# Splitting the gated activations behind the value rows, and a last normalization scaled by VectorE alone

## The chip, the cores and the metric

The kernel runs on one core of a Trainium2 chip. The metric is the device time of one execution in microseconds (us), taken as the median of several runs. Engines are named as the profile names them: PE is TensorE (PEld its weight loads), DVE is VectorE, ACT is ScalarE, POOL is GpSimd, SP is SyncE, which here only issues transfers. Transfers run on 16 DMA engines. SBUF is the memory on the core that all engines read, PSUM the one into which TensorE adds up.

## The reference

One decoder layer over 256 tokens of width 2048, in fp32. The change lies in its last part, a lookup of experts (PEER) and the normalization behind it. Each token has 8 heads; each picks the best 16 of 128 x 128 experts, and an expert is a single neuron with one row of `u` and one of `v`:

```python
    ue = u[eidx]
    h = jnp.einsum('cd,chkd->chk', xc, ue).astype(jnp.float32)
    a = jax.nn.gelu(h, approximate=False) * g
    ve = v[eidx]
    return jnp.einsum('chk,chkd->cd', a.astype(ve.dtype), ve)
...
    # the layer ends with
    x <- LayerNorm(ALPHA * x + PEER(x))
```

`a` is called the gated activation below: the gelu of a token's product with an expert's row, times the gate `g`. What lies ahead (a combined projection, two attentions, an output projection and a first normalization) is not touched.

## The kernel before, in words

**Products in fp32.** A matrix product is made from parts: a number is cast to a short form (the high part: `wh`, `ah`) and the rest is a subtraction (the low part: `wl`, `al`). ScalarE casts, VectorE subtracts, and TensorE adds up high x high, low x high and high x low. The helper `split` (L146) does both for small tiles, `split_half` for 1024 of the 2048 columns of a row tile.

**Experts in blocks.** Experts that tokens chose are put into columns: a block is 128 experts, one per partition, whose rows of `u` or `v` (128x2048, 1.049 MB) POOL gathers by a list of indices. Where a block serves both token tiles (t = 0 and 1, 128 tokens each) it is worked with all 256 tokens, else with the half that needs it. Blocks have a part: C and D, and the "singles" S0 and S1 (28 of them), in which each expert serves exactly one token.

**Units.** The program is a list of units; each needs one row tile of 1.049 MB. `run_units` works through them in order. The last 110 are the value units (rows of `v`), numbered u0 to u109 here; u0 begins near 1220 us. Their order alternates: a block for both tiles (24 matmuls of 128x512), then a single (8 matmuls) or a block for one tile (12 matmuls), with some changes; u101 is the last that adds to tile t = 0, and u102 to u109, the tail, are blocks of one half for t = 1. TensorE adds all of it up in eight banks of PSUM, four for each t. A unit has four steps s = 0 to 3, one for each 512 columns.

**What each unit needs, and who makes it.**

- its rows, `raw` or `rawv` (three buffers each, used in turn), gathered up to six units ahead on POOL (`dma_unit`); then `wh` by ScalarE and `wl` by VectorE in two halves, one unit ahead (`split_ahead`, called at each step; the halves are due at s = 0 and s = 2).
- its activations: `ar` comes from DRAM (`load_a`: SP for blocks of C, POOL's gather for D) and the gates `gr` by a gather on POOL, both four units ahead. `split_a(k + 2)`, called at s = 0, multiplies `ar` by `gr` on VectorE, casts it to `ah` on ScalarE and subtracts `al` on VectorE; for a single it writes the mask `one` instead, which says which token each expert serves.
- a single also needs its activations `acts`: the generator `job_singles` gathers its row of `u` and its token's row (`sr`, 1.049 MB each, four buffers, so two singles at a time), multiplies and sums them on VectorE, and, once per seven singles, gathers seven tiles of gates (`gsr`) and reduces them on VectorE to `gate` and `token`.

**What sets the order.** The program's order on each engine is the order in which Python calls the instructions; nothing is reordered later. All compute goes through a wrapper (`Paced`), so that every compute instruction has line L116; gathers have L187. The wrapper also keeps a model clock for each engine while the program is written down. Background work (`job_singles`; `job_ln2`, the normalization of tile t = 0) consists of generators. After each step, `pump` advances them if the clocks allow it: not if the model's ScalarE or VectorE is too far ahead of its TensorE, and not before the job's own due time. So a call that is made at another place in a step moves the clocks, and with them the places of the jobs' instructions. An engine works strictly in its order; an instruction that waits holds up all behind it, on POOL and SP the transfers' issues.

**The end.** When the last block of a tile has been added up, `residual` adds the four banks to ALPHA times the layer's input (`yacc`) and takes statistics of each 512 columns (`bn_stats`). `ln_stats` combines them (`bn_aggr`) and makes the reciprocal square root with small instructions. The scaling of 512 columns is either `ln2_a` and `ln2_b` (two VectorE instructions) or `ln2_pool` (one on ScalarE, two on POOL); each ends with the output's transfer. For t = 0 `job_ln2` takes columns 2 and 3 with VectorE and 0 and 1 with ScalarE and POOL. For t = 1, behind all units, the order before is: `ln_stats`, one scalar product (`ln2_start`), column block 3 by ScalarE and POOL, blocks 1, 2 and 0 by VectorE. The names `g2b2` are the normalization's weights, broadcast to two buffers of `sr`.

Of the kernel before, what the change touches and what calls it, by code (L numbers as in the profile page):

```python
# [17 lines left out]
OP = mybir.AluOpType  # L18
AX = mybir.AxisListType

P = 128
S = 256
# [99 lines left out]
def layer_kernel(ctx: ExitStack, tc: tile.TileContext, xT, x, win, wo, wq, ut, un, v, lams, sublng,  # L122
# [6 lines left out]
    SP = nc.sync  # L129
# [32 lines left out]
    units = []  # L162
# [60 lines left out]
    def split_ahead(k, s):  # L223
        if k + 1 < len(units) and units[k + 1]["kind"] == "C":
            turn_quarter(k + 1, s)
        for at, ahead, i in units[k]["at"]:
            if at == s and k + ahead < len(units) and units[k + ahead]["kind"] != "C":
                split_half(k + ahead, i)
# [3 lines left out]
    def start(gen):  # L232
        jobs.append([0.0, gen])
# [34 lines left out]
    def run_units(upto, slack=SLACK):  # L268


        while pos["k"] < upto:
            k = pos["k"]
            if k == 0:
                load_first()
                for _ in range(2):
                    dma_unit()
                for i in range(2):
                    split_half(1, i)
            if k == 2:
                load_consts()  # L280
            if k == 4:
                make_consts()
            u = units[k]
            clk["now"] = clk["PE"]
            n_late = len(later)
            for s, _ in enumerate(u["use"](u)):
                if s == 0:
                    if k >= n_c - 4:
                        load_a(k + 4)
                    while st["dma"] <= min(k + (6 if "vx" in keep else 3), len(units) - 1):  # L290
                        dma_unit()
                    if k >= n_c - 2:
                        split_a(k + 2)
                split_ahead(k, s)
                for f in later[:n_late]:
                    f()
                del later[:n_late]
                pump(slack)
                clk["now"] = clk["PE"]
                n_late = len(later)  # L300
            pos["k"] = k + 1
# [455 lines left out]
    def ln_stats(pool, t):  # L757

        mv[t] = pool.tile([P, 2], F32, name="mv", tag=f"mv{t}")
        rstd[t] = r = pool.tile([P, 4], F32, name="rstd", tag=f"rstd{t}")  # L760
        v, y, m, w = (r[:, i:i + 1] for i in range(4))
        DVE.bn_aggr(out=mv[t], in_=bst[t])
        DVE.tensor_scalar(v, mv[t][:, 1:2], EPS, None, op0=OP.add)
        DVE.tensor_scalar(y.bitcast(I32), v.bitcast(I32), 1, None, op0=OP.logical_shift_right)
        DVE.tensor_scalar(m, v, -0.5, None, op0=OP.mult)
        DVE.tensor_scalar(y.bitcast(I32), y.bitcast(I32), -1.0, RSQRT_MAGIC, op0=OP.mult, op1=OP.add)
        for _ in range(3):
            DVE.scalar_tensor_tensor(w, y, m, y, op0=OP.mult, op1=OP.mult)
            DVE.scalar_tensor_tensor(y, w, 1.5, y, op0=OP.add, op1=OP.mult)
# [462 lines left out]
    def cols_of(halves):  # L1232
        return slice(halves[0] * P, (halves[-1] + 1) * P)
# [116 lines left out]
                gather(u["a"], hd, hidx[:, c:c + 1])  # L1350
            gather(u["g"], gtab, column(aidx, u["part"], u["b"]))

    def split_a(k):
        if k >= n_all:
            return
        u = units[k]
        if u["kind"] == "S":
            u["ah"] = ex.tile([P, P], F32R, name="one", tag="one", bufs=2)
            DVE.tensor_scalar(u["ah"], row, token[:, u["s"]:u["s"] + 1], None, op0=OP.is_equal)
            return  # L1360
        u["ah"] = ex.tile([P, S], F32R, name="ah", tag="ah", bufs=3)
        u["al"] = ex.tile([P, S], F32R, name="al", tag="al", bufs=3)
        c = cols_of(u["halves"])
        DVE.tensor_tensor(u["a"][:, c], u["a"][:, c], u["g"][:, c], op=OP.mult)
        split(u["ah"][:, c], u["al"][:, c], u["a"][:, c])

    yps = {}
# [1 line left out]
    def use_v(n, single, halves):  # L1369
        def use(u):  # L1370
            for t in halves:
                if t not in yps:
                    yps[t] = [psA() if t == 0 else psB() for _ in range(4)]
            h, l = u["h"], u["l"]
            for c in range(4):
                vs = slice(c * 512, (c + 1) * 512)
                for t in halves:
                    ts = slice(t * P, (t + 1) * P)
                    o = (n == first_of[t], n == last_of[t])
                    if single:  # L1380
                        ops = ((u["ah"], h), (u["ah"], l))
                    else:
                        ops = ((u["ah"][:, ts], h), (u["ah"][:, ts], l), (u["al"][:, ts], h))
                    for i, (a, z) in enumerate(ops):
                        PE.matmul(yps[t][c], a, z[:, vs], start=o[0] and i == 0, stop=o[1] and i == len(ops) - 1)
                    if o[1]:
                        residual(t, c, yps[t][c])
                        if t == 0 and c == 3:
                            start(job_ln2())
                yield  # L1390
        return use

# [19 lines left out]
    def ln2_a(t, db):  # L1412
        y = ycols(t, db)
        c = slice(db * 512, (db + 1) * 512)
        DVE.scalar_tensor_tensor(y, y, mv[t][:, 0:1], g2b2[0][:, c], op0=OP.subtract, op1=OP.mult)

    def ln2_b(t, db):
        y = ycols(t, db)
        c = slice(db * 512, (db + 1) * 512)
        DVE.scalar_tensor_tensor(y, y, rstd[t][:, 1:2], g2b2[1][:, c], op0=OP.mult, op1=OP.add)  # L1420
        SP.dma_start(out[t * P:(t + 1) * P, c], y)

    def ln2_start(t):

        DVE.scalar_tensor_tensor(rstd[t][:, 2:3], mv[t][:, 0:1], -1.0, rstd[t][:, 1:2], op0=OP.mult, op1=OP.mult)

    def ln2_pool(t, db):
        y = ycols(t, db)
        c = slice(db * 512, (db + 1) * 512)
        ACT.activation(y, y, AF.Identity, scale=rstd[t][:, 1:2], bias=rstd[t][:, 2:3])  # L1430
        POOL.tensor_tensor(y, y, g2b2[0][:, c], op=OP.mult)
        POOL.tensor_tensor(y, y, g2b2[1][:, c], op=OP.add)
        (ACT if t else SP).dma_start(out[t * P:(t + 1) * P, c], y)

    def job_ln2():
        yield
        ln_stats(ex, 0)
        ln2_start(0)
        while not g2b2:
            yield  # L1440
        for db in (2, 3):
            yield
            ln2_a(0, db)
            ln2_b(0, db)
        while st["dma"] < n_all or st["a"] < n_all:
            yield
        for db in range(2):
            ln2_pool(0, db)
            yield
# [110 lines left out]
    keep["vx"] = ctx.enter_context(tc.tile_pool(name="vx", bufs=1, side="right"))  # L1560
    run_units(n_all, SLACK_VALUES)
    drain()
    ln_stats(ex, 1)
    ln2_start(1)
    ln2_pool(1, 3)
    for db in (1, 2):
        ln2_a(1, db)
    for db in (1, 2):
        ln2_b(1, db)
    ln2_a(1, 0)  # L1570
    ln2_b(1, 0)


    again = nc.values_load(flag[0:1, 0:1], min_val=0, max_val=1)
# [98 lines left out]
```

## Time and profile before

| what | value |
|---|---|
| median of 3 runs | 1713.2 us (1708.8 to 1714.13) |
| profiled execution | 1714.49 us, span 1712.4 us, mean granted clock 0.96 |
| PE busy | 1580.7 us, 92% of the span |
| DVE, ACT, POOL busy | 1285.7, 815.8, 599.5 us |
| moved by DMA | 409.19 MB, mean 239 GB/s |

The span is the time from the profile's first to its last instruction. Busy shares are means over stages that have different limits: the value units begin near 1220 us and the last matmul ends near 1693, and of these stretches of 100 us and less are shown below. In the rows of a timeline the first two numbers are the start and the duration in us; "x2" says that two instructions of a kind were put together; what stands in brackets at the end is how long the engine was idle before, and whose end released it. In the rows of waits the numbers are: us in total, times, the longest one.

### The profile page before, as it was taken

Reading aid. Unit: us, or ns where it says so; the run is one execution under the profiler, and the core shown is the slowest. Engines: PE = TensorE matmul, PEld = TensorE weight load, DVE = VectorE, ACT = ScalarE, POOL = GpSimd, SP = SyncE. Lnnn points to the kernel's source line nnn. Section 1 sums busy time; section 2 is a strip of 40 time slices with the busy share of each in tenths; the row PEclk is TensorE's granted clock in tenths of the full one; section 3 lists DMA queues with packets and bytes.
Section 4 is the critical chain, followed back from the end, with each engine's and each line's share of the span. In section 5 each row is a group of like instructions: output and inputs, shape, how many; then the busy total and the mean of one; then the engine's idle time right before and its main releaser. Section 6 shows DMA issues by size and latency. Waiting matters only on the chain.

```text
span 1712.4 us, 25292 instructions
## 1 busy us (share of the span) xinstructions
PE 1580.7 (92%) x9151; PEld 1334.9 (78%) x9151; DVE 1285.7 (75%) x2908; ACT 815.8 (48%) x1370; POOL 599.5 (35%) x557
## 2 busy tenths in 40 slices
PE   7999999998999899969798889999889999999994
PEld 5888888876888688759687778898858777788872
DVE  5686767665999898867956567776768888877767
ACT  5445555445433575315544324344445555555533
POOL 0033100004878500001010143344466666556742
PEclk9999999998999899979899899999999999999998
DMA  7454454555444446825147688798999999988861
GB/s 278 163 183 141 155 175 149 217 197 186 162 148 155 175 140 224 280 83 185 55 139 240 203 321 321 264 384 324 376 352 406 390 385 388 371 325 310 302 253 56
DMA packets 112532, 409.19 MB, mean 239 GB/s; under 512 B 11216, under 2 KB 62608, under 8 KB 69648
## 3 DMA queue, kind: packets, MB, share of 16 engines
q0 software_dynamic: 37856, 246.96, 38.0%
q1 hardware_dynamic: 74400, 160.27, 27.4%
q8 instruction: 74, 1.21, 0.3%
q14 instruction: 58, 0.48, 0.1%
q10 hardware_dynamic: 144, 0.26, 0.0%
HBM read 376.00 MB, written 31.39 MB: 238 GB/s over the span
## 4 chain that ended last, share of the span: by engine, by line
PE 67%; DVE 19%; DMA 5%; issue 3%; ACT 3%; POOL 1%; SPq 0%; DVEq 0%; ACTq 0%; POOLq 0%
PE psa L116 34%; PE psb L116 34%; DVE wl L116 6%; DVE oh L116 2%; ACT wh L116 2%; DVE og L116 1%; DVE lw L116 1%; DMA raw<-in_v_dram,vidx 1%; DVE ti L116 1%; DVE yacc L116 1%; DMA raw<-in_win_dram 1%; DMA raw<-in_un_dram,vidx 1%; DVE tv L116 1%; DVE eid L116 1%; DVE cand L116 1%
## 5 line engine op out<-in xcount | busy, mean ns | idle before, releaser
L116 PE MATMUL psb<-xx,wh 128*128 128x512 f32 (+1 forms) x1407 | 510.6, 397 | 0.3 <-issue 0.3
L116 DVE TENSOR_TENSOR wl<-raw,wh 128x1024 fp32r<-128x1024 f32 (+2 forms) x278 | 321.7, 1172 | 104.2 <-ACT wh L116 97.6
L116 PE MATMUL psb<-xx,wl 128*128 128x256 f32 x1392 | 376.7, 285 | 3.8 <-DVE wl L116 2.1
L116 ACT CAST wh<-raw 128x1024 fp32r<-128x1024 f32 (+1 forms) x278 | 283.6, 1045 | 69.2 <-PE psa L116 26.4
L116 PEld LDWEIGHTS psb<-xx,wh 128*128 128x128 f32 x1407 | 270.7, 194 | 37.6 <-issue 0.5
L116 PE MATMUL psa<-xx,wh 128*128 128x512 f32 x800 | 289.1, 405 | 9.3 <-DVE xx L116 8.0
L116 PEld LDWEIGHTS psb<-xx,wl 128*128 128x128 f32 x1392 | 269.8, 194 | 8.5 <-DVE wl L116 2.4
L187 POOL DMA_INDIRECT raw<-in_un_dram,vidx x54 | 59.6, 1103 | 457.8 <-PE psa L116 242.6
L116 PE MATMUL psa<-xx,wl 128*128 128x256 f32 x800 | 218.3, 283 | 1.0 <-DVE wl L116 0.8
L116 DVE TENSOR_TENSOR wl<-psa,wh 128x512 fp32r<-128x512 f32 x216 | 146.7, 687 | 89.3 <-ACT wh L116 78.5
L116 ACT CAST wh<-psa 128x512 fp32r<-128x512 f32 x216 | 126.7, 589 | 161.4 <-PE psa L116 145.2
L116 PEld LDWEIGHTS psa<-xx,wh 128*128 128x128 f32 x800 | 149.9, 191 | 42.8 <-ACT wh L116 9.9
L116 PEld LDWEIGHTS psa<-xx,wl 128*128 128x128 f32 x800 | 152.8, 191 | 7.0 <-DVE wl L116 2.4
L116 DVE TENSOR_TENSOR wl<-rawv,wh 128x1024 fp32r<-128x1024 f32 x106 | 125.7, 1222 | 28.4 <-ACT wh L116 22.5
L116 PE MATMUL psa<-ident,raw 128*128 128x128 f32 x864 | 133.1, 276 | 5.4 <-DMA raw<-in_un_dram,vidx 4.3
L116 ACT CAST ah<-ar 128x256 fp32r<-128x256 f32 (+1 forms) x82 | 30.3, 370 | 203.1 <-DVE ar L116 174.1
L116 PE MATMUL psb<-wl,ah 128*128 128x512 f32 x276 | 110.4, 400 | 7.2 <-DVE wl L116 7.2
L116 PEld LDWEIGHTS psa<-ident,raw 128*128 128x128 f32 x864 | 105.0, 143 | 15.0 <-issue 6.3
L116 PE MATMUL psa<-wh,ah 128*128 128x512 f32 x268 | 107.1, 400 | 5.1 <-ACT wh L116 5.1
L116 PE MATMUL psb<-wh,ah 128*128 128x512 f32 x276 | 110.3, 400 | 1.5 <-DVE bl L116 0.8
L116 PE MATMUL psa<-wl,ah 128*128 128x512 f32 x268 | 107.7, 402 | 4.1 <-DVE wl L116 3.2
L116 PE MATMUL psb<-wh,al 128*128 128x512 f32 x276 | 109.4, 396 | 0.0
(303 smaller groups left out, 2948.6 us busy)
## 6 DMA issues: line engine op xcount, KB each, us to landing
raw<-in_win_dram SPq DMA_DIRECT2D x42, 1024.0 KB
raw<-in_ut_dram SPq DMA_DIRECT2D x32, 1024.0 KB
raw<-in_wo_dram SPq DMA_DIRECT2D x18, 1024.0 KB
raw<-in_wq_dram SPq DMA_DIRECT2D x16, 1024.0 KB
gtab<-stg SPq DMA_DIRECT2D x32, 512.0 KB
cdr<-bl SPq DMA_DIRECT2D x39, 128.0 KB
ar<-cdr SPq DMA_DIRECT2D x39, 128.0 KB
hd<-bl SPq DMA_DIRECT2D x32, 128.0 KB
```

Source lines behind the costliest of these rows:

```text
L116: return f(*a, **k)
L187: nc.gpsimd.indirect_dma_start(dst, None, src, bass.IndirectOffsetOnAxis(ap=index, axis=0))
```

## The change

The function `split_a` is cut in two. `gated` (at s = 0, as before) holds the product `ar` x `gr` or a single's mask; `split_a`, with the cast `ah` and the subtraction `al`, is called at s = 2 behind `split_ahead`, so that it stands behind both halves of the row split made in that unit. `ln_stats` for t = 1 is called directly behind the last `residual`. All of tile t = 1 is scaled by VectorE, a block's two instructions one behind the other, and the outputs of blocks 1 and 3 are issued by ScalarE. The number of matmuls and their order do not change.

```diff
@@ run_units
                     if k >= n_c - 2:
-                        split_a(k + 2)
+                        gated(k + 2)
                 split_ahead(k, s)
+                if s == 2 and k >= n_c - 2:
+                    split_a(k + 2)
                 for f in later[:n_late]:
                     f()
@@
-    def split_a(k):
+    def gated(k):
         if k >= n_all:
             return
         u = units[k]
...
             DVE.tensor_scalar(u["ah"], row, token[:, u["s"]:u["s"] + 1], None, op0=OP.is_equal)
             return
+        c = cols_of(u["halves"])
+        DVE.tensor_tensor(u["a"][:, c], u["a"][:, c], u["g"][:, c], op=OP.mult)
+
+    def split_a(k):
+        if k >= n_all or units[k]["kind"] == "S":
+            return
+        u = units[k]
         u["ah"] = ex.tile([P, S], F32R, name="ah", tag="ah", bufs=3)
         u["al"] = ex.tile([P, S], F32R, name="al", tag="al", bufs=3)
         c = cols_of(u["halves"])
-        DVE.tensor_tensor(u["a"][:, c], u["a"][:, c], u["g"][:, c], op=OP.mult)
         split(u["ah"][:, c], u["al"][:, c], u["a"][:, c])
@@ use_v
                         if t == 0 and c == 3:
                             start(job_ln2())
+                        elif c == 3:
+                            ln_stats(ex, 1)
@@ ln2_b
-        SP.dma_start(out[t * P:(t + 1) * P, c], y)
+        (ACT if t and db % 2 else SP).dma_start(out[t * P:(t + 1) * P, c], y)
@@ behind run_units(n_all, SLACK_VALUES)
     drain()
-    ln_stats(ex, 1)
-    ln2_start(1)
-    ln2_pool(1, 3)
-    for db in (1, 2):
+    for db in range(4):
         ln2_a(1, db)
-    for db in (1, 2):
         ln2_b(1, db)
-    ln2_a(1, 0)
-    ln2_b(1, 0)
```

What this does to the order on the engines is seen at three places. The first is POOL at the start of the value units: `raw` and `rawv` are the units' rows, `gr` the gates of a block, `gsr` the seven gate tiles of a group of singles. Before:

```order
L187 DMA raw<-in_v_dram,vidx 128x2048
L187 DMA gr<-gtab,aidx 128x256
L187 DMA rawv<-in_v_dram,vidx 128x2048
L187 DMA gsr<-gtab,gi 128x128 x7
L187 DMA gr<-gtab,aidx 128x256
L187 DMA raw<-in_v_dram,vidx 128x2048
```

and after the change:

```order
L187 DMA raw<-in_v_dram,vidx 128x2048
L187 DMA rawv<-in_v_dram,vidx 128x2048
L187 DMA gsr<-gtab,gi 128x128 x7
L187 DMA raw<-in_v_dram,vidx 128x2048
L187 DMA gr<-gtab,aidx 128x256
L187 DMA rawv<-in_v_dram,vidx 128x2048
```

The group's seven gathers have moved ahead of two rows (those of u7 and u8) and one `gr`, and on VectorE its reduces stand two units earlier, ahead of the mask of u5 where they stood ahead of the gated product of u8.

The second place is POOL further on, from the rows of u11 to those of u15 (the `sr` pairs are a single's row of `u` and its token's row). Before:

```order
L187 DMA raw<-in_v_dram,vidx 128x2048
L187 DMA gr<-gtab,aidx 128x256
L187 DMA rawv<-in_v_dram,vidx 128x2048
L187 DMA gr<-gtab,aidx 128x256
L187 DMA raw<-in_v_dram,vidx 128x2048
L187 DMA gr<-gtab,aidx 128x256
L187 DMA rawv<-in_v_dram,vidx 128x2048
L187 DMA sr<-in_un_dram,vidx 128x2048
L187 DMA sr<-x1d,xidx 128x2048
L187 DMA raw<-in_v_dram,vidx 128x2048
```

and after the change, where the first pair stands ahead of the row of u11:

```order
L187 DMA sr<-in_un_dram,vidx 128x2048
L187 DMA sr<-x1d,xidx 128x2048
L187 DMA raw<-in_v_dram,vidx 128x2048
L187 DMA gr<-gtab,aidx 128x256
L187 DMA rawv<-in_v_dram,vidx 128x2048
L187 DMA sr<-in_un_dram,vidx 128x2048
L187 DMA sr<-x1d,xidx 128x2048
L187 DMA gr<-gtab,aidx 128x256
L187 DMA raw<-in_v_dram,vidx 128x2048
L187 DMA gr<-gtab,aidx 128x256
L187 DMA rawv<-in_v_dram,vidx 128x2048
L187 DMA sr<-in_un_dram,vidx 128x2048
```

Three pairs begin where one stood. Counted up to the row of u24, two of the last seven pairs stood ahead of it before, and all seven do now; from u52 on the two orders have the same pairs behind them.

The third place is VectorE at the end of the tail. `yacc_10161` is tile t = 0, `yacc_10162` tile t = 1; the gated product is that of u109, the last unit. Before:

```order
L116 TENSOR_TENSOR ar<-ar,gr 128x128
L116 TENSOR_TENSOR al<-ar,ah 128x128
L116 TENSOR_TENSOR wl<-raw,wh 128x1024 x2
L116 SCALAR_TENSOR_TENSOR yacc_10162<-yacc_10162,psb 128x512
...
L116 BN_STATS bst_16549<-yacc_10162 128x6
L116 SCALAR_TENSOR_TENSOR yacc_10161<-yacc_10161,mv,sr 128x512
L116 SCALAR_TENSOR_TENSOR yacc_10161<-yacc_10161,rstd,sr 128x512
L116 BN_AGGR mv<-bst_16549 128x2
```

and after the change:

```order
L116 TENSOR_TENSOR al<-ar,ah 128x128
L116 SCALAR_TENSOR_TENSOR yacc_10161<-yacc_10161,mv,sr 128x512
L116 SCALAR_TENSOR_TENSOR yacc_10161<-yacc_10161,rstd,sr 128x512
L116 TENSOR_TENSOR ar<-ar,gr 128x128
L116 TENSOR_TENSOR wl<-raw,wh 128x1024 x2
L116 TENSOR_TENSOR al<-ar,ah 128x128
L116 SCALAR_TENSOR_TENSOR yacc_10162<-yacc_10162,psb 128x512
L116 BN_STATS bst_16556<-yacc_10162 128x6
```

`al` stands behind both `wl`, the last scalings of t = 0 stand ahead of the last unit's gated product, and `bn_aggr` comes directly behind the four pairs of `residual`. On ScalarE the two scalings of t = 0 that feed POOL stood behind everything of u109; now the first stands ahead of its casts `wh` and the second behind its `ah`.

## The prediction

> **What bounds the kernel now.** I read first the stretches with their busy times (columns: stretch in us, its length, busy us of PE, PEld, DVE, ACT and POOL with instructions, granted clock, DMA share, GB/s), and then the page's chain of waits.
>
> ```profile
> 1200.00:1300.00 100.00, 86.63 (x438) 71.32 (x438) 70.96 (x100) 44.92 (x72) 58.88 (x51) 0.93 0.94 370
> 1300.00:1400.00 100.00, 99.86 (x427) 79.71 (x426) 81.89 (x106) 55.89 (x72) 62.34 (x53) 1.00 0.99 392
> 1400.00:1500.00 100.00, 99.13 (x423) 78.85 (x423) 81.70 (x105) 58.11 (x73) 64.66 (x53) 1.00 0.97 381
> 1500.00:1600.00 100.00, 100.00 (x430) 80.46 (x429) 74.98 (x95) 57.19 (x69) 62.87 (x58) 1.00 0.88 315
> 1660.00:1713.00 53.00, 24.75 (x92) 16.27 (x90) 38.47 (x71) 15.41 (x21) 11.51 (x9) 0.85 0.20 69
> ...
> PE 67%; DVE 19%; DMA 5%; issue 3%; ACT 3%; POOL 1%; SPq 0%; DVEq 0%; ACTq 0%; POOLq 0%
> ```
>
> The value units run from about 1220 to 1693. From 1300 to 1600 TensorE has hardly a hole: 427 matmuls in 100 us, one per 0.234 us. So a unit takes 24 x 0.234 = 5.6 us with both halves, 2.8 with one, and 1.9 as a single (8 matmuls). In the same stretch the DMA engines are busy to 0.99, at 392 GB/s: two resources are full at once, and the rows arrive just as fast as they are used. Only the first 100 us and the last 50 hold idle TensorE time. The change moves work in all three places, so each gets a term.
>
> **Term 1: the rows of the singles come earlier.** The split's new place in the program changes when the background job of the singles is advanced, and the listing of POOL's order shows where that ends: of the last seven singles' row pairs, two stood ahead of the expert row of value unit 24, and now all seven do. That is 5 x 2 x 1.049 = 10.5 MB pushed in front of rows that TensorE needs first. What the trace says of them:
>
> ```profile
> L187 POOL DMA_INDIRECT sr<-x1d,xidx x7: 938/1039/1966, 1280.5 to 1429.4; - x7
> ...
> 1265.74 0.94 POOL L187 DMA_INDIRECT rawv<-in_v_dram,vidx  x1 [0.30 <-DVE al L116]
> 1279.73 2.00 ACT L116 CAST wh<-rawv 128x1024 fp32r<-128x1024 f32 x2
> 1317.35 0.94 POOL L187 DMA_INDIRECT rawv<-in_v_dram,vidx  x1 [1.93 <-DVE ar L116]
> 1338.67 1.99 ACT L116 CAST wh<-rawv 128x1024 fp32r<-128x1024 f32 x2
> ...
> 1452.25 6.52 DMA rawv<-in_v_dram,vidx
> ...
> 1285.00:1290.00 5.00, 5.00 (x24) 4.00 (x23) 3.59 (x6) 2.55 (x5) 2.39 (x4) 1.00 1.02 418
> ```
>
> The first row spreads the seven pairs over 1280 to 1429. The next four are issue and first use of the rows of unit 10 and of unit 24: 14.0 and 21.3 us apart. A transfer that was waited for took 6.5 us, so these rows lay ready for 7.5 and 14.8 us. Two ways to the loss, with 405 GB/s, the middle of 392 (sustained) and 418 (the best stretch). First, by demand: two neighbouring units and one single's pair need 2 x 1.049 + 2.097 MB, and about 0.39 MB of gates and activations (1.5 x 0.262), 4.59 MB or 11.3 us; TensorE has 34 matmuls for it, 7.9 us (a unit with both halves, and the mean of a single and a one-half unit). Seven times the 3.4 us between them is 23.8; less the 7.5 that lie ready at unit 10 it is 16.3. Second, by lateness: 10.5 MB take 25.9 us, less the 14.8 that unit 24 had to spare is 11.1. I take 15, nearer the first, because the second leaves out that POOL issues in order: the buffers of the pairs are four, so the third pair waits for VectorE to consume the first, and the gates and rows behind it on POOL wait too. TensorE is full in every later stretch, so the loss is not made good, though the DMA has less to do from there on. Bounds: +4 (418 GB/s by the second way, 25.1, and all 21.3 of unit 24 to spare) and +26.5 (392 GB/s, 11.7 against 7.9 us seven times, nothing ready).
>
> The Trainium skill, "DMA: Bandwidth & Descriptors", section "Where 436 GB/s comes from", says that for transfers between memory and SBUF the memory side binds at about 358 GB/s for a core. By that figure 4.59 MB take 12.8 us and the term is 34.3 - 7.5 = +27. The row with 392 GB/s over 100 us contradicts it, so I keep 405.
>
> **Term 2: the start.** The reduces of the second group of gathered gates move two units forward, ahead of unit 5 in place of unit 8.
>
> ```profile
> 1268.62 1.08 DVE L116 TENSOR_REDUCE gate<-gsr 128x7 f32<-128x896 f32 x1
> 1272.26 0.42 DVE L116 TENSOR_TENSOR ar<-ar,gr 128x256 f32<-128x256 f32 x1
> ...
> PE psa L116 <- ACT wh L116: 5.1, 3, 3.7
> ...
> 1275.00:1280.00 5.00, 4.62 (x11) 3.66 (x12) 4.53 (x7) 2.69 (x5) 4.12 (x3) 0.50 1.02 415
> ```
>
> They hold VectorE from 1268.62 to 1272.26, 3.64 us, with the gated product of unit 8 behind them; TensorE then waits up to 3.7 us (the waits between 1230 and 1300), and runs the next 5 us at half clock, 11 matmuls where 24 fit: at most 13 x 0.234 = 3.0 more. If the reduces had cover two units earlier, 6.7 us would go; but rows land late there too (singles' pairs now stand ahead of unit 2's), and the same block then hits unit 5 or 6. I take 0, bounds -6.7 and +3.6 (the reduces once more on the path).
>
> **Term 3: the tail.** In the last eight units, of one half each, VectorE sets the pace:
>
> ```profile
> PE psb L116 <- DVE wl L116: 7.2, 8, 1.7
> ...
> 1673.57 0.28 DVE L116 TENSOR_TENSOR ar<-ar,gr 128x128 f32<-128x128 f32 x1
> 1674.29 0.29 DVE L116 TENSOR_TENSOR al<-ar,ah 128x128 fp32r<-128x128 f32 x1 [0.44 <-ACT ah L116]
> 1675.24 2.36 DVE L116 TENSOR_TENSOR wl<-rawv,wh 128x1024 fp32r<-128x1024 f32 x2 [0.66 <-ACT wh L116]
> 1677.52 0.28 DVE L116 TENSOR_TENSOR ar<-ar,gr 128x128 f32<-128x128 f32 x1
> ...
> 1676.52 0.50 PE L116 MATMUL psb<-wl,ah 128*128 128x512 f32 x1 [0.76 <-DVE wl L116]
> ```
>
> From gate to gate is 3.95 us against TensorE's 2.8. Of it 0.44 waits for ScalarE's cast of the activations, and 0.66 for the cast of the rows, which ScalarE does behind the first. With `al` last, the row casts no longer stand behind the activations' cast and both waits vanish: 2.85 us. Seven periods save 7 x 1.10 = 7.7, as much as TensorE waits there. The last unit pays: its `al` (0.29, and a start-up of some 0.15) now follows `wl`, +0.45. What stood in the unit's first wait is now covered by the 2.36 us of `wl`.
>
> ```profile
> 1689.38 1.52 ACT L116 ACTIVATE yacc<-yacc,rstd 128x512 f32<-128x512 f32 x2
> 1690.28 5.72 POOL L116 TENSOR_TENSOR yacc<-yacc,sr 128x512 f32<-128x512 f32 x4 [19.16 <-ACT yacc L116]
> 1690.84 0.68 DVE L116 SCALAR_TENSOR_TENSOR yacc<-yacc,psb 128x512 f32<-128x512 f32 x1
> 1694.79 0.67 DVE L116 SCALAR_TENSOR_TENSOR yacc<-yacc,psb 128x512 f32<-128x512 f32 x1
> 1696.11 0.73 DVE L116 SCALAR_TENSOR_TENSOR yacc<-yacc,mv,sr 128x512 f32<-128x512 f32 x1
> 1697.54 0.26 DVE L116 BATCH_NORM_AGGREGATE mv<-bst 128x2 f32<-128x24 f32 x1
> 1699.74 0.16 DVE L116 SCALAR_TENSOR_TENSOR rstd<-mv,rstd 128x1 f32<-128x1 f32 x1
> 1699.82 1.41 DVE L116 SCALAR_TENSOR_TENSOR yacc<-yacc,mv,sr 128x512 f32<-128x512 f32 x2
> 1701.14 3.42 DVE L116 SCALAR_TENSOR_TENSOR yacc<-yacc,rstd,sr 128x512 f32<-128x512 f32 x2
> 1700.83 3.19 POOL L116 TENSOR_TENSOR yacc<-yacc,sr 128x512 f32<-128x512 f32 x2 [4.83 <-ACT yacc L116]
> 1705.26 0.75 DVE L116 SCALAR_TENSOR_TENSOR yacc<-yacc,rstd,sr 128x512 f32<-128x512 f32 x1
> ```
>
> The other token tile's last pair of scalings (1696.11 to 1697.54, 1.43 us) moves ahead of the last gate: it costs the same there, 0. The end itself: from 1699.82 to 1706.01 before, 6.19 us; VectorE alone takes four such pairs, 4 x 1.43 = 5.72, and the 0.08 to the next start of the scalar product goes too: -0.55. What the cover hid: POOL's four products lay beside additions that read PSUM, which kept their 0.67 us. Beside products that read SBUF twice, two VectorE instructions took 3.42 where 0.75 each is usual: (3.42 - 1.50) / 2 = 0.96 us per POOL product. In the changed order ScalarE comes to those two scalings before the last row casts, so POOL's products fall beside `wl`, which also reads SBUF twice. Three of the four: +2.9 (bounds 0 and 3.8). The last outputs issued from ScalarE find their engine idle: 0. Sum -7.7 + 0.45 + 2.9 - 0.55 = -4.9; bounds -7.8 and -4.0.
>
> By the Trainium skill, "SBUF — State Buffer", section "SBUF: two separate sides", VectorE with two SBUF inputs and GpSimd share a port pair as an exclusive lock for a whole instruction. Then each product costs up to its own 1.43 us (5.72 / 4), four cost 5.7, and the tail saves only 2.1; the row with 0.96 is nearer and stays.
>
> **The sum.** 15 + 0 - 4.9 = +10. The profiled execution took 1714.49, the median is 1713.2: 1724 and 1723. I say **1724**.
>
> **Rivals.** *The lead covers it.* No byte is added; if the transfers of the pairs fill gaps and the rows that lie ready (14.8 us at unit 24) grow enough meanwhile, term 1 is 0. With term 3 alone the time is 1709; with the start's 6.7 gone too, 1702. For it speaks that six row buffers stand behind TensorE; against it the DMA share of 0.99, which leaves no gap to fill. It decides the sign as soon as term 1 is below 5.
>
> *Nothing covers it.* The pairs block POOL's queue from the first on and the rows' lead is used up at once: term 1 is 23.8 to 26.5, and each wait of TensorE brings slow matmuls as at 1275. 1714.5 + 24 - 5 = 1733, up to 1739 with the reduces on the path (+3.6) and the tail at -4.
>
> *The tail gives nothing.* POOL's products block `wl`, and TensorE waits for `al` in each unit instead (0.45 x 8 = 3.6): the tail saves 0.5 at most, 1714.5 + 15 - 0.5 = 1729.
>
> **How the numbers follow.** The forecast has 0.55 and spans 1713 to 1731 by itself; the lead covers it 0.17, nothing covers it 0.16, the tail gives nothing 0.12. About 0.3% (5 us) is what a measurement of this kernel can tell from no change. Faster, below 1708: 0.17, most of the first rival and the forecast's edge. Within: 0.11. Slower: 0.72. Leaving a tenth out on either side, the range is 1708 to 1737.
>
> **What would show it.** Term 1: the first and last `sr` gathers lie within some 70 us, not 150, and between 1290 and 1350 TensorE's busy share falls well below 99% with waits on rows or gates, while the DMA share falls in 1400 to 1500. Term 2: where TensorE first waits over 3 us. Term 3: 2.85 us from gate to gate, `wl` of the last two units stretched beside POOL, `BATCH_NORM_AGGREGATE` directly behind the last statistics, and 5.7 us of scaling. I am wrong if TensorE stays at 99% from 1300 on, or if its waits come from something other than rows and gates.

## The result: 1.1% slower

| | before | changed |
|---|---|---|
| median | 1711.5 us (5 runs, 1708.8 to 1714.1) | 1729.1 us (5 runs, 1728.2 to 1731.1) |
| span of the profiled execution | 1712.4 us | 1727.2 us |
| last matmul of u10 ends | 1290.9 | 1290.8 |
| from there to the last matmul of u101 | 368.2 us | 388.2 us |
| from there to the end of the span | 53.4 us | 48.2 us |

The ratio is 1.0108, with a 95% interval of 1.0095 to 1.0121. 1724 us was forecast, with a range of 1708 to 1737: 11 us of loss on the median then known, 17.6 measured. The last three rows cut the spans of the two profiled executions, which differ by 14.8 us, at the places where the prediction's three terms end: the start costs nothing, the middle 20.0 us, and the tail gives back 5.2.

### The profile page after: what moved, and what is told of

Read it like the earlier page. It is cut to its first block, busy times and chain, and to the rows that moved or that the text cites. A ratio compares the mean times of both kernels' runs of the same rounds, so it can differ in the third digit from the quotient of the medians.

```text
span 1727.2 us, 25259 instructions
## 1 busy us (share of the span) xinstructions
PE 1588.2 (92%) x9151; PEld 1340.5 (78%) x9151; DVE 1277.6 (74%) x2909; ACT 815.1 (47%) x1369; POOL 639.3 (37%) x555
## 4 chain that ended last, share of the span: by engine, by line
PE 62%; DVE 21%; DMA 7%; issue 5%; POOL 2%; ACT 2%; DVEq 0%; SPq 0%; ACTq 0%; POOLq 0%
PE psa L116 32%; PE psb L116 30%; DVE wl L116 5%; DVE oh L116 3%; DMA sr<-x1d,xidx 2%; DVE og L116 2%; DMA gr<-gtab,aidx 2%; DMA raw<-in_v_dram,vidx 2%; DVE lw L116 1%; ACT wh L116 1%; POOL gsr L187 1%; POOL sr L187 1%; DVE tv L116 1%; DVE ti L116 1%; DVE eid L116 1%
## 5 line engine op out<-in xcount | busy, mean ns | idle before, releaser
L116 PE MATMUL psa<-wh,al 128*128 128x512 f32 x268 | 109.5, 408 | 13.4 <-DVE al L116 13.4
L187 POOL DMA_INDIRECT raw<-in_v_dram,vidx x57 | 93.8, 1646 | 69.0 <-DVE wl L116 30.6
L187 POOL DMA_INDIRECT gr<-gtab,aidx x82 | 103.1, 1257 | 38.9 <-issue 21.3
L116 ACT CAST wh<-rawv 128x1024 fp32r<-128x1024 f32 x106 | 106.1, 1044 | 23.4 <-issue 15.4
```

The costliest lines, as they stand in the source:

```text
L116: return f(*a, **k)
L187: nc.gpsimd.indirect_dma_start(dst, None, src, bass.IndirectOffsetOnAxis(ap=index, axis=0))
```

## The profile after

The stretches of the changed kernel, with the columns of those shown of before:

```profile
1285.00:1360.00 75.00, 62.32 (x227) 46.48 (x226) 53.29 (x71) 31.13 (x44) 45.06 (x36) 0.91 1.02 412
1300.00:1400.00 100.00, 88.83 (x351) 68.57 (x350) 72.13 (x96) 47.19 (x63) 60.53 (x46) 0.95 0.98 390
1400.00:1500.00 100.00, 100.00 (x430) 80.47 (x429) 72.60 (x94) 57.90 (x70) 67.95 (x49) 1.00 0.84 308
1500.00:1600.00 100.00, 100.00 (x431) 80.43 (x430) 71.81 (x96) 56.88 (x69) 73.82 (x55) 1.00 0.85 310
```

The first of these stretches in the kernel before:

```profile
1285.00:1360.00 75.00, 75.00 (x323) 60.06 (x322) 60.92 (x80) 42.22 (x55) 44.60 (x40) 1.00 1.00 399
```

The whole loss lies ahead of 1360: there TensorE issues 227 matmuls in 75 us where 323 fit. The DMA engines are full in both kernels, at 412 GB/s here and 399 before. From 1400 on TensorE has no hole and the DMA share falls to 0.84: the bytes that came early are missing later, where nothing waited for them. The singles' gathers, what VectorE waits for between 1285 and 1362 (us in all, times, longest), and TensorE's largest sum of waits there:

```profile
L187 POOL DMA_INDIRECT sr<-x1d,xidx x7: 939/1158/1374, 1267.6 to 1329.8; - x7
...
DVE ar L116 <- DMA gr<-gtab,aidx: 15.4, 5, 5.3
DVE sr L116 <- DMA sr<-x1d,xidx: 7.9, 3, 4.8
...
PE psa L116 <- DVE al L116: 11.0, 6, 3.2
```

In the kernel before, the same stretch of VectorE shows:

```profile
DVE wl L116 <- ACT wh L116: 5.5, 10, 0.7
DVE al L116 <- ACT ah L116: 5.2, 12, 0.5
DVE wl L116 <- DMA rawv<-in_v_dram,vidx: 1.3, 2, 0.7
```

The seven pairs stand within 62 us where they took 149, and VectorE, which had waited half a microsecond at a time for ScalarE, now waits 23.3 us for transfers: for gates first, then for the singles' own rows. One such wait, as a chain over three engines:

```profile
1293.02 1.03 POOL L187 DMA_INDIRECT sr<-in_un_dram,vidx  x1 [0.30 <-issue]
1294.36 1.16 POOL L187 DMA_INDIRECT sr<-x1d,xidx  x1 [0.30 <-issue]
1295.83 0.95 POOL L187 DMA_INDIRECT gr<-gtab,aidx  x1 [0.30 <-issue]
...
1305.50 0.41 DVE L116 TENSOR_TENSOR al<-ar,ah 128x256 fp32r<-128x256 f32 x1
1310.57 0.29 DVE L116 TENSOR_TENSOR ar<-ar,gr 128x128 f32<-128x128 f32 x1 [4.66 <-DMA gr<-gtab,aidx]
1310.78 1.22 DVE L116 TENSOR_TENSOR wl<-raw,wh 128x1024 fp32r<-128x1024 f32 x1
1311.91 2.29 DVE L116 SCALAR_TENSOR_TENSOR sr<-sr 128x2048 f32<-128x2048 f32 x1
...
1314.12 1.22 DVE L116 TENSOR_TENSOR wl<-raw,wh 128x1024 fp32r<-128x1024 f32 x1
1315.26 0.29 DVE L116 TENSOR_TENSOR al<-ar,ah 128x128 fp32r<-128x128 f32 x1
...
1315.60 0.50 PE L116 MATMUL psa<-wh,al 128*128 128x512 f32 x1 [3.05 <-DVE al L116]
```

POOL issues a pair and right behind it the gates of u15. These are 0.13 MB at most, but VectorE gets them 14.7 us later, after 4.66 us of idling. Then the next single's product (2.29 us) runs between the halves of `wl`, `al` comes last, and TensorE has waited 3.05 us for it.

The tail, from the gated product of u107 to the last scaling:

```profile
1693.81 0.28 DVE L116 TENSOR_TENSOR ar<-ar,gr 128x128 f32<-128x128 f32 x1
...
1696.48 0.28 DVE L116 TENSOR_TENSOR ar<-ar,gr 128x128 f32<-128x128 f32 x1
...
1699.15 1.78 DVE L116 SCALAR_TENSOR_TENSOR yacc<-yacc,mv,sr 128x512 f32<-128x512 f32 x1
1700.97 1.67 DVE L116 SCALAR_TENSOR_TENSOR yacc<-yacc,rstd,sr 128x512 f32<-128x512 f32 x1
...
1702.77 2.35 DVE L116 TENSOR_TENSOR wl<-raw,wh 128x1024 fp32r<-128x1024 f32 x2
1705.04 1.34 DVE L116 TENSOR_TENSOR al<-ar,ah 128x128 fp32r<-128x128 f32 x1
...
1711.93 0.69 DVE L116 BATCH_NORM_STATS2 bst<-yacc 128x6 f32<-128x512 f32 x1
1712.66 0.26 DVE L116 BATCH_NORM_AGGREGATE mv<-bst 128x2 f32<-128x24 f32 x1
...
1714.76 0.75 DVE L116 SCALAR_TENSOR_TENSOR yacc<-yacc,mv,sr 128x512 f32<-128x512 f32 x1
...
1719.89 0.75 DVE L116 SCALAR_TENSOR_TENSOR yacc<-yacc,rstd,sr 128x512 f32<-128x512 f32 x1
...
1697.95 4.14 POOL L116 TENSOR_TENSOR yacc<-yacc,sr 128x512 f32<-128x512 f32 x2 [8.70 <-ACT yacc L116]
1704.03 3.56 POOL L116 TENSOR_TENSOR yacc<-yacc,sr 128x512 f32<-128x512 f32 x2 [1.93 <-ACT yacc L116]
```

From gate to gate is 2.67 us where it was 3.95. Beside POOL's products three VectorE instructions are stretched: the first tile's two scalings (1.78 and 1.67 in place of 0.75) and the last `al` (1.34 in place of 0.28).

## The experiments

In all tables, "middle" is from the end of u10's last matmul to that of u101, and "tail" from there to the end of the span, both read from each run's profile in the same way. One part of the tail varies for a reason that no run shows: from the end of VectorE's last scaling to the end of the span it is 4.9 to 5.2 us in e3, e4 and e7, and 6.4 to 6.8 in all others.

**Pace and place taken apart.** The change does two things to the middle: it puts `ah` and `al` later, and through the model clocks it puts the singles earlier. The first two runs make the other two of the four combinations.

```diff
+HOLD = {20: -1, 21: 2, 22: 13, 23: 19, 24: 25, 25: 32, 26: 38, 27: 45, 28: 51}
@@ job_singles of the changed kernel (e1); of the kernel before with the changed kernel's units (e2)
-            while pos["k"] < single_turn(i):
+            while pos["k"] < max(single_turn(i), n_c + HOLD.get(i, -99)):
                 yield
...
@@ run_units, e2 alone
-                pump(slack)
+                pump(None if n_c - 2 <= k < n_c + 21 else slack)
```

> The changed kernel, with the background job of the singles held so that each of its gathers, reduces and products is issued at the unit at which the kernel before issues it; the split's new place and the new end stay. Theory (the loss is the singles' rows, pulled ahead of rows and gates that TensorE needs first): the 20 us lost between u10 and u24 are gone, TensorE is busy 99% or more from 1300 on, and the tail's gain of 5 us is left: 1706 to 1708, a ratio of about 0.997. Rival (the split's new place itself: al stands last on VectorE, behind whatever waits there, and TensorE waits for al): the waits for al stay, 11 us or more of them, and the ratio stays at 1.006 or above.

> The kernel before, split and end as they were, with the job of the singles advanced so that its gathers and products are issued at the units at which the changed kernel issues them. Theory: the same loss of 15 to 20 us between u10 and u24 as in the changed kernel, with no gain in the tail: 1727 to 1733, ratio 1.009 to 1.012. Rival (the split's place): TensorE stays full, within 4 us of the kernel before, ratio 0.998 to 1.002.

| | singles as before | singles early |
|---|---|---|
| split as before | before: middle 368.2, tail 53.4 | e2: middle 386.3, tail 53.4; ratio 1.0103 (1.0086 to 1.0120) |
| split behind the rows | e1: middle 365.9, tail 48.1; ratio 0.9953 (0.9937 to 0.9970) | changed: middle 388.2, tail 48.2 |

Both rivals fall. From 1150 us on, POOL's 270 gathers stand in e1 in the same order as in the kernel before, and in e2 in the same order as in the changed kernel. The early singles cost 18.1 us with the old split and 22.3 with the new one. With the singles as before, the new place of the split gains 2.3 us in the middle; with early singles it loses 1.9. The tail gains 5.3 in e1. The row of 1300 to 1400, first of the changed kernel with the old pace, then of the kernel before with the new pace:

```profile
1300.00:1400.00 100.00, 100.00 (x430) 80.42 (x430) 83.12 (x112) 57.97 (x74) 69.22 (x54) 1.00 1.02 409
```

```profile
1300.00:1400.00 100.00, 90.20 (x351) 69.31 (x352) 74.25 (x95) 50.25 (x66) 53.04 (x45) 0.93 0.98 380
```

TensorE is full in the one, with the split that was changed, and has lost as many matmuls as in the changed kernel (351) in the other, with the split that was not.

**Bytes or the order on VectorE.** The early singles bring bytes, and also products that stand between the halves of `wl`.

```diff
@@ job_singles of the changed kernel
-                bufs[i] = [ex.tile([P, D], F32, name="sr", tag="sr", bufs=4) for _ in range(2)]
+                bufs[i] = [ex.tile([P, D], F32, name="sr", tag="sr", bufs=4) for _ in range(2)][:1] * 2
                 gather(bufs[i][0], un, column(vidx, f"S{t}", b))
-                gather(bufs[i][1], x1d, xidx[:, s:s + 1])
```

> The changed kernel without the gather of each single's token row: only the row of u is gathered, and VectorE multiplies it with itself (a single's activation is then another number; all else is computed). Every instruction on VectorE, ScalarE and TensorE stands at its place and takes as long; one gather of 1.049 MB in each pair is gone. Theory (bytes in front of rows and gates): ahead of u24 stand 5.2 MB more than in the kernel before instead of 10.5 plus what the two other pairs save, 9 MB less than in the changed kernel or 22 us of transfer, so the lead covers it: u10 to u101 in 366 to 371 us where the changed kernel took 388. Rival (the order on VectorE: the singles' products between the halves of wl, each waiting for its rows, and al behind them): 380 us or more.

The middle took 369.6 us, within the theory's 366 to 371, with every product at its place. So without half the bytes the order on VectorE costs 3.7 us at most, against the 365.9 of e1, whose split stands at the same place. The run also takes one issue for each single off POOL, and cannot tell that from the bytes. (One execution; its time was 1697.1 us, since half the pairs' bytes are gone ahead of u10 too, which ended at 1277.9.)

**Gates or rows.** VectorE waited mostly for gates. In the program's order they are gathered four units ahead and used two units ahead, so they have two units to arrive; the rows have four. In the trace of the kernel before, 12.7 to 15.4 us passed between issue and use of the gates of u11 to u24, and 18.8 to 21.3 for their rows.

```diff
@@ run_units of the changed kernel
-                        load_a(k + 4)
+                        load_a(k + 5)
```

> The changed kernel with activations and gates loaded five units ahead in place of four, from the same four buffers, so that each gather of gates stands ahead of one row and mostly one single's pair more in POOL's order. No byte less is moved. If late gates are what costs (VectorE waits 15 us for them between 1290 and 1362), the loss between u10 and u24 falls by 6 us or more and the ratio to 1.007 or less. If the bytes cost and the gates are only what is waited for first, the waits move to rows and products, and the ratio stays between 1.009 and 1.012.

```profile
DVE sr L116 <- DMA sr<-x1d,xidx: 19.0, 6, 4.2
DVE ar L116 <- DMA gr<-gtab,aidx: 0.9, 1, 0.9
```

These are VectorE's waits between 1285 and 1362 in that run. The waits for gates fell from 15.4 to 0.9 us, those for the singles' rows rose from 7.9 to 19.0. The ratio was 1.0089 (1.0073 to 1.0106) and the middle 385.0: 3.2 of the 20 us are gone. With the gates in time, the singles' rows were late in their place.

**The tail by itself.** The late split for the last eight units alone (e3), and with the first tile's POOL scalings held until the last unit (e4):

```diff
@@ run_units of the changed kernel
                         gated(k + 2)
+                        if k + 2 < n_all - TAIL:
+                            split_a(k + 2)
                 split_ahead(k, s)
-                if s == 2 and k >= n_c - 2:
+                if s == 2 and k + 2 >= n_all - TAIL:
@@ job_ln2, e4 alone
-        while st["dma"] < n_all or st["a"] < n_all:
+        while st["dma"] < n_all or st["a"] < n_all or pos["k"] < n_all - 1:
```

> The changed kernel, with the split moved behind the rows' split only for the last eight units; ahead of them it stands where it stood before, and so do the singles. Theory: nothing changes until the tail, and the tail gives what it gave in the changed kernel, 5 us: ratio 0.997. Rival (part of the tail's gain comes from the late split in the units ahead of it): 2 us or less, ratio 0.999 or above.

> As the run with the tail alone, and in addition the two scalings of the first token tile that feed POOL are held until the last unit is being worked on, so that POOL's four products come beside the additions that read PSUM again. Theory (those products held up VectorE by 1.0 us for each of its two scalings of the first tile and for the last al, 3.0 us in all): another 2 to 3 us, so 7 to 8 us under the kernel before, ratio 0.9955. Rival (the products were only moved and now hold up the last tile's scaling instead): no gain against the tail alone.

e3: ratio 0.9972 (0.9957 to 0.9987), middle 368.2, tail 46.7, 6.7 us less than before. Of these, 1.2 lie behind VectorE's last scaling; up to it the gain is 5.4, as in the changed kernel (5.3). e4: ratio 0.9946 (0.9929 to 0.9963), tail 44.7; the 2.0 less than in e3 come from the hold. The two scalings and the `al` of e4:

```profile
1675.13 0.75 DVE L116 SCALAR_TENSOR_TENSOR yacc<-yacc,mv,sr 128x512 f32<-128x512 f32 x1
1675.91 0.75 DVE L116 SCALAR_TENSOR_TENSOR yacc<-yacc,rstd,sr 128x512 f32<-128x512 f32 x1
...
1679.05 1.35 DVE L116 TENSOR_TENSOR al<-ar,ah 128x128 fp32r<-128x128 f32 x1
...
1678.05 6.16 POOL L116 TENSOR_TENSOR yacc<-yacc,sr 128x512 f32<-128x512 f32 x4 [12.84 <-ACT yacc L116]
```

The scalings are back at 0.75, which is the 2.0 us; the last `al` still meets a product of POOL.

**The end by itself.** The changed end on the kernel before, with the split's call put back to s = 0:

```diff
@@ run_units of the changed kernel
                         gated(k + 2)
+                        split_a(k + 2)
                 split_ahead(k, s)
-                if s == 2 and k >= n_c - 2:
-                    split_a(k + 2)
```

> The kernel before with the changed end alone: statistics combined directly behind the last residual, the last tile scaled by VectorE alone, two outputs issued by ScalarE; the split stands where it stood before. Theory: from the start of the last residual addition to the end of the span 0.5 us less than before, and TensorE's last eight units unchanged, so a time within 3 us of the kernel before. Rival (VectorE alone is no faster than the three engines together): that stretch is equal or longer.

From the start of the last tile's first residual addition (1688.66) to the end of the last scaling (1703.46) it took 14.80 us, before 15.17 (1690.84 to 1706.01): 0.4 less. To the end of the span it took 19.7 against 21.6. The other 1.4 us lie behind VectorE's last instruction, which in the changed kernel is followed by 6.6 us and in the kernel before by 6.4; so that part is not a gain that the changed kernel shows. One execution, at 1711.3 us.

**Both gains together (e8)**: e1 and the hold.

> The changed kernel with the singles at the pace of the kernel before and with the first tile's two POOL scalings held until the last unit. Theory: the gains add up, 2.3 us of TensorE's waits in the value units, 7 to 9 us in the tail: ratio 0.993 to 0.995, about 1701. Rival (the two share the same waits of VectorE): no better than either alone, 0.9953 or above.

Ratio 0.9945 (0.9932 to 0.9959), middle 365.9, tail 46.1: the hold takes 2.0 us off e1's tail. On the ratio it cannot be told from e4, nor, as the intervals overlap, surely from e1. Its middle is 2.8 us shorter than e4's. Its tail is 1.4 longer, all of it behind VectorE's last scaling, which in both ends 39.4 us after u101.

**The same rule ahead of the middle.** If bytes cost where they stand in front of rows, fewer pairs ahead of u10 should help. In the kernel before, 21 pairs stand ahead of its row.

```diff
@@ job_singles of the changed kernel with the hold (e9; e10 has 17 and 7.0)
-            while pos["k"] < single_turn(i):
+            while pos["k"] < (single_turn(i) if i < 14 else n_c + 8 + 5.5 * (i - 14)):
                 yield
```

> The changed kernel with the first tile's POOL scalings held until the last unit, and with the last 14 singles (two groups) paced evenly through the value units, one for 5.5 units from u8 on; in the kernel before, the rows of 21 of the 28 pairs were gathered ahead of u10's row, here of 14. No byte is added or removed. Theory (a byte costs where it stands in front of rows that are needed while the DMA engines are full, and nothing where TensorE has the longer work): without 7 pairs (14.7 MB) the rows of u0 to u10 land earlier, u10 ends 8 to 13 us sooner (the run with half the bytes: 13 us), and from u10 to u101 it stays at 366 to 370 us, since 14 pairs in 100 units need 50 x 6.15 + 14 x 5.2 = 380 us of transfer at 405 GB/s where TensorE has 397: 1688 to 1693. Rival (the start's loss comes from VectorE's reduces and from the first rows' own transfers, not from the pairs): u10 ends where it does in the paced runs, 1283 to 1288, and the time stays at 1700.

> As the run with 14 singles spread, but with the last 11 only, one for 7 units from u8 on. Theory: a part of the same gain, 4 pairs (8.4 MB) less ahead of u10's row than before, u10 ends 4 to 8 us sooner, 1693 to 1697. Rival: 1700, as with 14.

| | pairs ahead of u10's row | u10 ends | middle | tail | ratio |
|---|---|---|---|---|---|
| e8 | 21 | 1282.6 | 365.9 | 46.1 | 0.9945 |
| e10 | 17 | 1264.4 | 381.7 | 46.1 | 0.9901 (0.9884 to 0.9918) |
| e9 | 14 | 1261.1 | 393.9 | 46.1 | 0.9960 (0.9944 to 0.9977) |

The start gained 18 and 21 us, more than forecast; the middle lost 16 and 28, which was not forecast, though by the sum of bytes there was room. e10, at 1694.1 us, is the fastest of all; that lies within its forecast of 1693 to 1697, but by luck, as two misses cancelled. Its middle loses at two places. VectorE's rows there:

```profile
1378.11 1.09 DVE L116 TENSOR_REDUCE gate<-gsr 128x7 f32<-128x896 f32 x1 [5.88 <-DMA gsr<-gtab,gi]
1558.48 0.29 DVE L116 TENSOR_TENSOR ar<-ar,gr 128x128 f32<-128x128 f32 x1 [11.69 <-DMA gr<-gtab,aidx]
```

The first waits for the second group's gathered gates; the second for gates that POOL issued behind a pair while SP loaded the two rows of normalization weights. The last two runs were to take these clumps apart.

```diff
@@ job_singles, e11 (e12 has 14 and 5.5)
-            while pos["k"] < (single_turn(i) if i < 17 else n_c + 8 + 7.0 * (i - 17)):
+            while pos["k"] < (single_turn(i) if i < 17 else n_c + 8 + 7.0 * (i - 17) - 3 * (i % SGRP == 0)):
...
                     yield 5000.0
+                    while pos["k"] > n_c and pos["k"] < n_c + 8 + 7.0 * (i - 17) + 2:
+                        yield
...
+        while pos["k"] < n_c + 96:
+            yield
         g2b2.extend(ex.tile([P, D], F32, name="sr", tag="sr", bufs=4) for _ in range(2))
```

> The run with 11 singles spread, with its two clumps of transfers taken apart: the last group's seven gate gathers are issued three units earlier and reduced five units after their issue instead of two, and the two rows of normalization weights (1.049 MB each) are loaded at u96 instead of u85, where they stood beside a single's pair (6.3 MB with the rows next to them, VectorE waited 11.7 us for gates behind them). Theory: TensorE's two lumps of waits there (5.6 and 3.5 us, with half-speed matmuls behind each, 11 us in all against the paced runs) go: u10 to u101 366 to 370 us, 1682 to 1687. Rival (the eleven pairs need the DMA engines' time wherever they stand): the waits come back at other units, 1692 to 1695.

> The run with 14 singles spread, with the clumps taken apart in the same way, both groups' gate gathers and the normalization weights. Theory: u10 some 3 us sooner than with 11, and the lumps gone, 1679 to 1685. Rival: three more pairs overfill the value units, and what the start gains is lost again: 1690 or above.

Both missed: ratios 0.9928 (0.9905 to 0.9950) and 1.0032 (1.0018 to 1.0046), middles 380.8 and 401.1. The second clump of e11 stayed, and its row says why; the transfers issued between 1530 and 1570 still hold the weights (median us to landing at the row's end):

```profile
sr<-in_ln2g_dram SPq DMA_DIRECT2D x1, 1024.0 KB, 9.5
sr<-in_ln2b_dram SPq DMA_DIRECT2D x1, 1024.0 KB, 14.6
...
1559.11 0.29 DVE L116 TENSOR_TENSOR ar<-ar,gr 128x128 f32<-128x128 f32 x1 [9.93 <-DMA gr<-gtab,aidx]
```

The load was moved to u96 in the program, but SP issued it at 1542.1, while TensorE was at u79, as soon as its buffers came free (the row is in the last section). So this part of the edit changed nothing on the chip. At the first clump the waits moved from the group's gates to those of three units (3.9, 2.0 and 2.1 us). Whether the eleven pairs could be placed without loss is left open; e12 shows that fourteen, so placed, could not.

## Why the prediction was right, and where it was off

**Term 1, the singles' rows: the mechanism was right, the size too small.** 15 us were taken, 20.0 measured in the middle, made of 22.3 for the early singles and -2.3 for the split's place in units ahead of the tail, which the prediction had costed at nothing. The demand of seven pairs was worked out as 23.8 us, and that is the measured size to 1.5 us. What failed is the subtraction, "less the 7.5 that lie ready at unit 10". That lead was read off the value rows, and rightly (in e3, u10's row was used 14.0 us after its issue and landed after 6.5), but the first thing to be late was the gates, and behind them VectorE stood still whatever rows lay ready. The run e3 has the order of the kernel before up to the tail, and its trace has some landings. For u18 it shows the issue of the row, its time to landing and its first use, then the same of the gates:

```profile
1293.13 2.00 POOL L187 DMA_INDIRECT rawv<-in_v_dram,vidx  x1 [1.92 <-DVE one L116]
rawv<-in_v_dram,vidx POOLq DMA_INDIRECT x1, 8.3
1313.12 1.04 ACT L116 CAST wh<-rawv 128x1024 fp32r<-128x1024 f32 x1
...
1299.61 1.04 POOL L187 DMA_INDIRECT gr<-gtab,aidx  x1 [0.30 <-issue]
gr<-gtab,aidx POOLq DMA_INDIRECT x1, 10.2
1312.35 0.42 DVE L116 TENSOR_TENSOR ar<-ar,gr 128x256 f32<-128x256 f32 x1
```

The row lay ready for 11.7 us, the gates for 2.5. With 2.5 in place of 7.5 the sum gives 21.3, an estimate made afterwards. The second way, 10.5 MB less unit 24's 14.8 us, was off for the same reason and gave half. Of the runs, the one with half the bytes (369.6) shows that the bytes decide. The one with gates a unit earlier (385.0) shows that the gates' short lead accounts for 3.2 us by itself; with it gone, the singles' own rows set the next limit.

The rule on the memory side's 358 GB/s (the Trainium skill, "DMA: Bandwidth & Descriptors", section "Where 436 GB/s comes from") would have given +27. The trace does not agree: 22.3 was measured, and 412 GB/s were moved between 1285 and 1360, so the row stays the better guide.

**Term 2, the start: 0 was forecast, -0.1 measured.** The reduces moved ahead of u5, and VectorE waited there for the group's gates:

```profile
1256.41 1.09 DVE L116 TENSOR_REDUCE gate<-gsr 128x7 f32<-128x896 f32 x1 [7.56 <-DMA gsr<-gtab,gi]
```

u10's end differs by 4.6 us among the kernel before and the three runs with its order up to there (1286.3 to 1290.9), so no smaller effect can be read from one profile; that the forecast was met to 0.1 us is luck. (By the trace, u0 begins at 1231.3 before and at 1230.2 after the change, not near 1220.)

**Term 3, the tail: -4.9 forecast, -5.2 measured.** Gate to gate fell to 2.67 us, below TensorE's 2.8 (2.85 forecast). POOL's cost was forecast as three products at 0.96, 2.9 us; the three stretched rows show 1.03, 0.92 and 1.06, 3.0. The place was wrong: not `wl`, which kept its 2.35, but the first tile's scalings and `al`. The pair of scalings costed at 1.43 and "0" there is what took most of it. The end was forecast at -0.55; the run of the end alone shows 0.4 up to VectorE's last instruction. TensorE's last matmul came only 2.2 us sooner, counted from u101; the rest of the gain lies behind it, where the pair had stood.

**The rivals.** "The lead covers it" fell by TensorE's 351 matmuls in 1300 to 1400. "Nothing covers it" named the right size for the singles (24, against 22.3); its other part, the block of POOL's queue from the first pair on, is not what the rows show: between 1262 and 1333 POOL never idled for more than 1.7 us ahead of an issue, while the DMA engines were full (1.01 to 1.02 from 1275 on) and what it issued was used late. Single issues took POOL up to 4.6 us (about 1 is usual); no run takes that time apart from the bytes. "The tail gives nothing" fell: 5.2 us.

How the loss divides between TensorE's plain waits and slow matmuls can be estimated from the rows of 1285 to 1360. TensorE stood idle for 12.7 us (75 less 62.3). The 227 matmuls filled 62.3 us where they need 52.7 at the pace of before, so 9.6 us went into slow matmuls (granted clock 0.91, before 1.00).

## What to carry to other kernels

Where transfers and TensorE are both full, the order of transfers is a cost of its own: here bytes that moved ahead were paid at once (22.3 us) and given back where nobody waited. The lead that counts is the shortest one among the inputs of a unit, here the small gates' (2.5 us for u18), not that of the large rows (11.7); once it is longer, the next shortest counts. And where a model clock decides when background work is written down, an edit to the foreground is also an edit to that work: holding the singles at their old pace turned this change from 1.1% slower to 0.5% faster.

## What the runs showed of the hardware that was not expected

VectorE and POOL took turns, a whole instruction at a time. The two `wl` at 1702.77 kept their 2.35 us though POOL's pair began at 1704.03; that pair took 3.56 us where two products take 2.86 (5.72 / 4 each), and the `al` behind `wl` took 1.34 in place of 0.28. Read so, POOL waited until `wl` had ended, and `al` waited for POOL's product. The Trainium skill, "SBUF — State Buffer", section "SBUF: two separate sides", says just that of VectorE with two SBUF inputs: whoever starts first has the port pair for its whole instruction. The trace agrees. By the rule a product costs up to its own 1.43 us; the stretches of 1.03, 0.92 and 1.06 are 0.4 to 0.5 us short of that, and what made the difference is not shown.

SP ran ahead of the place at which its issue was written: the loads of e11, written at u96, went out in u79. SP had issued nothing since 1502.2. In e10, where they are written eleven units earlier, they went out at 1539.8, in u79 too. In e11 that was the instant at which the single's product that read their buffers had ended (the product's two rows, then SP's):

```profile
1539.82 2.28 DVE L116 SCALAR_TENSOR_TENSOR sr<-sr 128x2048 f32<-128x2048 f32 x1
1542.03 0.08 DVE L116 DVE_READ_ACCUMULATOR sr<-sr 128x1 f32 x1
1542.13 0.33 SPq L1410 DMA_DIRECT2D sr<-in_ln2g_dram  x1
```
